# A two-layer decoder trunk: the order of instructions taken from the tool's time-line simulator

## The chip, the cores and the metric

The kernel is one program on one core of a Trainium2 chip. Its time is the device time of one execution in microseconds (us). TensorE (PE) multiplies, VectorE (DVE) and ScalarE (ACT) work on tiles in on-chip memory, GpSimd (POOL) does a little, and SyncE (SP) issues almost all transfers from the chip's main memory. Each engine takes its own instructions strictly in the order in which they were written into its list; between engines, semaphores make an instruction wait for what it needs. So an instruction that waits holds up all that stand behind it on its engine.

## The reference, cut to what matters

```python
# x (1, 256, 2048), c (1, 2048); everything float32
for layer in range(2):
    mod = silu(c) @ ada_w[layer, 0] + ada_b[layer, 0]      # 2048 x 6144 per use, four uses
    shift, scale, gate = split(mod, 3)
    h = rms_norm(x) * (1 + scale) + shift
    y = mlstm_mixer(h, ...) if layer == 0 else rglru_mixer(h, ...)
    x = x + gate * y
    h, gate = ada_modulate(x, c, ada_w[layer, 1], ada_b[layer, 1])
    x = x + gate * (square(relu(h @ w1[layer])) @ w2[layer])   # 2048 x 8192 and back
return rms_norm(x) * final_g
# mlstm_mixer: h @ w_in gives q, k, v, an output gate o and two gate columns per head; 8 heads in
#   two chunks of 128 positions: decay weights from cumulative sums and running maxima of the gate
#   columns, scores q k^T times these weights, a state k^T v carried from chunk to chunk, a
#   denominator, an RMS norm per head; the result times sigmoid(o), @ w_out
# rglru_mixer: h @ w_in gives xb, gb; a causal convolution over 4 positions of xb; two gates per
#   block of 256 channels by small products; a linear recurrence over time; times gelu(gb); @ w_out
```

## The kernel before, in words

Activations lie transposed, 128 channels by 256 positions to a tile, 16 tiles for the model's width. Products run in a split form: a weight tile of 128 x 2048 (1 MB, `raw`) is loaded by SP into a pool of four buffers; ACT copies each half into a rounded high part (`whi`, L174) and DVE subtracts it to get the low part (`wlo`, L175), in pools of four halves each, so two weight tiles are split ahead of PE at most. Activations are split likewise into the two halves of a `pair` (L184 and L185, or L187 and L188). PE then multiplies high by high, high by low and low by high: `mm3` (L194 to L196, three matmuls of 128x256), `mm2` (L200, L201, one of 128x512 and one of 128x256) or `mmu` (L217 to L219). A `block` is one output tile: 16 channel tiles, 48 matmuls with `mm3`.

Beside this runs the conditioning: 192 tiles `adaraw` of about 1 MB, each reduced on DVE against the vector made from `c` (L127) to one column of shifts, scales or gates. They are spread over the program by pacing numbers in the code, and they use the same buffers as the weights or two extra ones.

The stages, in order of time: the norm of x and the first projection in five groups of channel tiles (`group`, L511; from group 1 on ACT first copies the partial sums back into PSUM at L526, and copies the result out at L537); the gate columns and their cumulative sums and maxima (L574 to L626), which are written to a small table in main memory (`rows_d`) and read back broadcast as one tile `MB` per head (L634); then the eight heads, with eight blocks of the output gate (`ogate`) placed among them by a table in the code; the output projection (the first four tiles together, `awoa`, then twelve blocks); the first MLP; the RG-LRU mixer, two of its eight channel blocks at a time; its output projection (`bwo`); the second MLP, and the last norm.

One head goes back and forth between the engines. ACT makes the weights `E` (L646) and `qw` (L652) from `MB`, and `kw` (L643) from PE's transposed key `kp`; PE makes the state `cp` (L661) which ACT copies to `Cn` (L664); PE makes `num` and `den` (L671 to L677); ACT scales and squares these (`hb` L685, `hsq` L688, `ad` L680), DVE takes a maximum (L681) and ACT squares it (L682); PE sums the squares (`hss` L693) and DVE adds (L695). After every second head the pair of heads is normed: a table load and a reciprocal root on ACT (`rsy`, L270), three steps and two products on DVE (L271 to L273, L727), and the split into `zhi` (ACT, L731) and `zlo` (DVE, L732), which the output projection reads. The buffers for these allow two heads to be under way.

In the RG-LRU mixer the small gate products `gacc` (L194 to L196 into the second PSUM pool of three buffers) are followed on ACT by `th` (L836), `aa` (L839) and `TT` (L841), a root (L860) and a Gelu (L862), each of these with a table load when the function set changes; then on DVE by L865 to L870 and the split into the pairs that `bwo` reads.

What sets the order: the program is written as if one instruction followed another, and the tool makes each engine's list from it at building time by a simulation in which ready instructions are taken by priority. The priority is the place in the program, moved up by 200 for the weight splits (L173) and by 50 for the conditioning tiles (L126), by 1000 for the first norms.

## Time and profile before

| what | value |
|---|---|
| time, median of 3 runs (lowest, highest) | 2244.34 us (2240.72, 2247.15) |
| time of the profiled execution | 2244.5 us |
| its span | 2242.8 us, so 1.7 us lie around the span |
| mean clock granted to TensorE | 0.989 of full |
| busy in the span: PE, DVE, ACT, POOL | 2181.7, 1722.3, 1286.1, 90.1 us |
| read from main memory | 596.93 MB, 267 GB/s over the span |

A busy PE is a PE with at least one matmul under way. Matmuls overlap, so that the mean duration of one (0.28 us for 128x256) is longer than the distance from start to start; where the text counts matmuls it uses distances or the number in a stretch. In the rows of waits and of the time line, the number in square brackets is the idle time of the engine just before the instruction, followed by what ended it.

### The profile page before, as it was taken

The numbers are of one execution on the slowest core, as the hardware profiler recorded it, in microseconds if no ns is written. First come the engines' busy times: TensorE is split into PE (matmuls) and PEld (weight loads), VectorE is DVE, ScalarE is ACT, GpSimd is POOL, SyncE is SP. The second block draws the span as 40 slices with busy tenths as digits, with TensorE's granted clock in tenths as the row PEclk, the third lists the DMA queues.
The fourth block names the chain that finished last, engine by engine and source line by source line (L and its number), as shares of the span: only waits on it lengthen the run. The fifth ranks groups of instructions, "written<-read, shape, count | busy, mean of one in ns | idle before, by whom it ended". The sixth has DMA issues, their size and how long they took to land.

```text
span 2242.8 us, 34191 instructions
## 1 busy us (share of the span) xinstructions
PE 2181.7 (97%) x13606; PEld 1960.5 (87%) x13606; DVE 1722.3 (77%) x2199; ACT 1286.1 (57%) x1997; POOL 90.1 (4%) x70
## 2 busy tenths in 40 slices
PE   7899899899999999999999999999999999999998
PEld 6798799788888889888889999889888889888887
DVE  6777888988898788888889988998875555555554
ACT  6677777345674335665445877756664334665443
POOL 0000010220000000000110000020000000000110
PEclk9999999899999999999999999999999999999999
DMA  8888887897788999998997665776875555555552
GB/s 345 348 325 319 307 300 255 303 337 270 285 284 319 337 322 332 328 334 319 322 335 276 211 229 208 269 276 238 307 284 203 188 188 188 188 188 188 189 188 93
DMA packets 88671, 601.25 MB, mean 268 GB/s; under 512 B 10424, under 2 KB 14648, under 8 KB 16192
## 3 DMA queue, kind: packets, MB, share of 16 engines
q1 hardware_dynamic: 86400, 598.03, 74.3%
q8 instruction: 106, 1.74, 0.3%
q10 hardware_dynamic: 2112, 1.05, 0.2%
q14 instruction: 53, 0.43, 0.1%
HBM read 596.93 MB, written 2.11 MB: 267 GB/s over the span
## 4 chain that ended last, share of the span: by engine, by line
PE 86%; DVE 7%; ACT 3%; issue 2%; DMA 1%; SPq 0%; DVEq 0%; ACTq 0%
PE mm L200 42%; PE mm L201 22%; PE mm L511 8%; DVE wlo L175 3%; PE mm L196 2%; PE mm L195 2%; PE mm L194 2%; DVE adaraw L127 2%; ACT whi L174 1%; PE mm L218 1%; PE mm L217 1%; PE mm L219 1%; DMA adaraw<-in_ada 1%; PE mm L357 0%; DVE hmod L311 0%
## 5 line engine op out<-in xcount | busy, mean ns | idle before, releaser
L200 PE MATMUL mm<-pair,whi 128*128 128x512 f32 x4272 | 1496.3, 394 | 5.0 <-DVE pair L188 3.2
L201 PE MATMUL mm<-pair,wlo 128*128 128x256 f32 x4272 | 1195.9, 280 | 0.8 <-DVE wlo L175 0.8
L175 DVE TENSOR_TENSOR wlo<-raw,whi 128x1024 fp32r<-128x1024 f32 x736 | 900.2, 1233 | 380.1 <-ACT whi L174 375.9
L174 ACT ACTIVATE whi<-raw 128x1024 fp32r<-128x1024 f32 x736 | 771.9, 1057 | 609.7 <-PE mm L200 476.7
L200 PEld LDWEIGHTS mm<-pair,whi 128*128 128x128 f32 x4272 | 802.6, 188 | 190.7 <-DVE pair L188 4.7
L201 PEld LDWEIGHTS mm<-pair,wlo 128*128 128x128 f32 x4272 | 804.7, 188 | 1.7 <-DVE wlo L175 1.1
L127 DVE SCALAR_TENSOR_TENSOR adaraw<-adaraw,cbc 128x2050 f32<-128x2050 f32 x192 | 439.7, 2291 | 50.7 <-DMA adaraw<-in_ada 41.7
L511 PE MATMUL mm<-pair,whi 128*128 128x256 f32 x736 | 136.0, 288 | 10.7 <-ACT pair L187 5.7
L511 PEld LDWEIGHTS mm<-pair,whi 128*128 128x128 f32 x736 | 115.8, 194 | 12.9 <-ACT pair L187 6.3
L194 PE MATMUL mm<-pair,whi 128*128 128x256 f32 x432 | 123.1, 285 | 0.0
L195 PE MATMUL mm<-pair,whi 128*128 128x256 f32 x432 | 122.0, 282 | 0.0
L196 PE MATMUL mm<-pair,wlo 128*128 128x256 f32 x432 | 121.4, 281 | 0.0
L511 PE MATMUL mm<-pair,wlo 128*128 128x256 f32 x368 | 104.0, 288 | 2.9 <-DVE wlo L175 2.9
L336 DVE SCALAR_TENSOR_TENSOR xall<-mm,mod,xall 128x256 f32<-128x256 f32 x170 | 81.0, 480 | 27.0 <-PE mm L201 18.7
L378 ACT ACTIVATE hsum<-hsum 128x256 f32<-128x256 f32 x121 | 49.2, 413 | 81.7 <-DVE hsum L261 71.3
L291 POOL TENSOR_TENSOR nacc<-nacc,nsq 128x256 f32<-128x256 f32 x52 | 75.6, 1453 | 351.0 <-ACT nsq L282 350.7
L196 PE MATMUL mm<-zhi,wlo 128*128 128x256 f32 x256 | 75.8, 296 | 6.6 <-DVE wlo L175 6.6
L194 PEld LDWEIGHTS mm<-pair,whi 128*128 128x128 f32 x432 | 81.9, 190 | 0.4
L194 PE MATMUL mm<-zhi,whi 128*128 128x256 f32 x256 | 74.9, 297 | 7.6 <-ACT zhi L731 5.5
L195 PEld LDWEIGHTS mm<-pair,whi 128*128 128x128 f32 x432 | 81.8, 189 | 0.0
L196 PEld LDWEIGHTS mm<-pair,wlo 128*128 128x128 f32 x432 | 81.8, 189 | 0.0
L511 PE MATMUL mm<-whi,pair 128*128 128x512 f32 x256 | 81.0, 394 | 0.0
(218 smaller groups left out, 2054.7 us busy)
## 6 DMA issues: line engine op xcount, KB each, us to landing
raw<-in_w SPq DMA_DIRECT2D x220, 1024.0 KB, 5.1
adaraw<-in_ada SPq DMA_DIRECT2D x192, 1025.0 KB, 6.6
raw<-in_wqkv SPq DMA_DIRECT2D x40, 1024.0 KB, 8.5
raw<-in_w1a SPq DMA_DIRECT2D x32, 1024.0 KB, 6.2
raw<-in_bwi SPq DMA_DIRECT2D x28, 1024.0 KB, 5.0
raw<-in_bwo SPq DMA_DIRECT2D x16, 1024.0 KB, 5.1
raw<-in_awo SPq DMA_DIRECT2D x12, 1024.0 KB, 5.5
raw<-in_wo SPq DMA_DIRECT2D x8, 1024.0 KB, 6.2
```

Of the source, the lines that this page charges most:

```text
L127: V.scalar_tensor_tensor(out=raw, in0=raw, scalar=1.0, in1=cbc, op0=ALU.mult, op1=ALU.mult, accum_out=mod[i][:, j:j + 1])
L174: A.activation(hi, sl, AF.Copy)
L175: V.tensor_tensor(out=lo, in0=sl, in1=hi.bitcast(F32), op=ALU.subtract)
L194: PE.matmul(out, lhsT=whi, rhs=hi, start=first, stop=False)
L195: PE.matmul(out, lhsT=whi, rhs=lo, start=False, stop=False)
L196: PE.matmul(out, lhsT=wlo, rhs=hi, start=False, stop=last)
L200: PE.matmul(out, lhsT=whi, rhs=p.rearrange("p a t -> p (a t)"), start=first, stop=False)
L201: PE.matmul(out[:, 0:S], lhsT=wlo, rhs=p[:, 0, :], start=False, stop=last)
L291: G.tensor_tensor(out=self.acc, in0=self.acc, in1=sq, op=ALU.add)
L336: V.scalar_tensor_tensor(out=xT[j], in0=acc[:, a:a + S], scalar=mod[i][:, 32 + j:33 + j], in1=xT[j], op0=ALU.mult, op1=ALU.add)
L378: A.activation(h, h, AF.Relu, bias=c)
L511: PE.matmul(out, lhsT=l, rhs=m, start=clear and kk + n == 0, stop=kk == gn - 1 and n == len(ops) - 1, skip_group_check=True)
```

## The change

The context in which the program is written gets one argument. It selects the other of the two simulators that the tool has for ordering: one that keeps queues and transfers on a time line. Instructions, tiles, buffers, pools and priorities are the same; only the order in each engine's list differs, and with it the places where ACT needs a new function table (40 loads instead of 37).

```diff
-    with tile.TileContext(nc) as tc:
+    with tile.TileContext(nc, schedule_with_timeline_sim=True) as tc:
         trunk_kernel(tc, *args)
```

Of PE's 13426 instructions 10585 stand at the same place in both lists; of DVE's 2009 it is 729, of ACT's 1997 it is 113, of SP's 586 it is 497. The MLPs, most of the time, have nearly the same order on PE. The larger moves are in the first projection, in the heads and at the end of the RG-LRU mixer.

SP, between the first group of the projection and the second (`raw` are weight tiles, `adaraw` conditioning tiles; a piece of the difference, with - for before and + for now):

```order
+L161 DMA raw_341<-in_wqkv 128x2048
+L161 DMA raw_386<-in_wqkv 128x2048
+L161 DMA raw_434<-in_wqkv 128x2048
 L125 DMA adaraw_338<-in_ada 128x2050
-L161 DMA raw_341<-in_wqkv 128x2048
 L125 DMA adaraw_383<-in_ada 128x2050
-L161 DMA raw_386<-in_wqkv 128x2048
+L161 DMA raw_531<-in_wqkv 128x2048
+L161 DMA raw_595<-in_wqkv 128x2048
 L125 DMA adaraw_428<-in_ada 128x2050
+L161 DMA raw_662<-in_wqkv 128x2048
 L125 DMA adaraw_431<-in_ada 128x2050
```

Weight tiles move ahead of conditioning tiles: before the last of the conditioning tiles that the second group needs (adaraw_503, the 24th transfer before), there now stand four more weight tiles.

PE, at the state of head 0 (`cp_2791`; mm_2796 and mm_3392 are output-gate blocks, the second and the seventh of eight). Before:

```order
L194 MATMUL mm_2796<-pair_233,whi_2799 128x256
L195 MATMUL mm_2796<-pair_233,whi_2799 128x256
L196 MATMUL mm_2796<-pair_233,wlo_2800 128x256
L661 MATMUL cp_2791<-v0_195,kw_2778 128x256
L662 MATMUL cp_2791<-ones_85,kw_2778 128x128
L194 MATMUL mm_2796<-pair_513,whi_2799 128x256
L195 MATMUL mm_2796<-pair_513,whi_2799 128x256
```

Now:

```order
L194 MATMUL mm_3392<-pair_2287,whi_3399 128x256
L195 MATMUL mm_3392<-pair_2287,whi_3399 128x256
L196 MATMUL mm_3392<-pair_2287,wlo_3400 128x256
L661 MATMUL cp_2791<-v0_195,kw_2778 128x256
L662 MATMUL cp_2791<-ones_85,kw_2778 128x128
L671 MATMUL num_2859<-E_2780,v0_195 128x128
L672 MATMUL num_2859<-E_2780,v1_196 128x128
L675 MATMUL den_2866<-E_2780,ones_85 128x128
```

`cp_2791` is PE's row 1255 before and row 1546 now: six output-gate blocks that lay among the heads stand ahead of head 0, and one (mm_3522) is left among them. The reads of `MB` come later with them: on SP, five weight tiles and five conditioning tiles that stood behind the write of `rows_d` now stand ahead of it, and one weight tile and two conditioning tiles, where there was one conditioning tile, between it and the first `MB`.

PE, at the first product of the RG-LRU mixer's output projection that reads the last blocks' results (`pair_14156`; mm_14166, mm_14219, mm_14275 and mm_14328 are the first four output tiles). Before:

```order
L200 MATMUL mm_14275<-pair_13536,whi_14282 128x512
L201 MATMUL mm_14275<-pair_13536,wlo_14283 128x256
L200 MATMUL mm_14275<-pair_13543,whi_14282 128x512
L200 MATMUL mm_14166<-pair_14156,whi_14173 128x512
L201 MATMUL mm_14166<-pair_14156,wlo_14174 128x256
L200 MATMUL mm_14219<-pair_14156,whi_14226 128x512
```

Now:

```order
L200 MATMUL mm_14328<-pair_14142,whi_14335 128x512
L201 MATMUL mm_14328<-pair_14142,wlo_14336 128x256
L200 MATMUL mm_14328<-pair_14149,whi_14335 128x512
L201 MATMUL mm_14328<-pair_14149,wlo_14336 128x256
L200 MATMUL mm_14166<-pair_14156,whi_14173 128x512
L201 MATMUL mm_14166<-pair_14156,wlo_14174 128x256
```

Between the last of the gate products (gacc_13999) and this place stood 94 matmuls before, and 40 now; the gate products have moved back behind the blocks that used to follow them.

## The prediction

> **What bounds the kernel now.** I read the page first: busy shares, then the chain of work that ended last.
>
> ```profile
> PE 2181.7 (97%) x13606; PEld 1960.5 (87%) x13606; DVE 1722.3 (77%) x2199; ACT 1286.1 (57%) x1997; POOL 90.1 (4%) x70
> PE 86%; DVE 7%; ACT 3%; issue 2%; DMA 1%; SPq 0%; DVEq 0%; ACTq 0%
> ```
>
> PE is idle for 2242.8 - 2181.7 = 61.1 us in all. No instruction is added or removed but three table loads on ACT, so the change can win at most those 61 us and what they cost in clock, and loses wherever the new order makes PE wait. The table of stretches says where PE has room:
>
> ```profile
> core 0: us, PE busy (x) PEld busy (x) DVE busy (x) ACT busy (x) POOL busy (x), PEclk, DMA share, GB/s
> 20.00:80.00 60.00, 48.46 (x281) 43.58 (x282) 44.19 (x48) 34.13 (x53) 0.00 (x0) 0.89 0.90 360
> 400.00:450.00 50.00, 42.85 (x307) 42.35 (x308) 45.25 (x59) 19.66 (x40) 14.04 (x8) 0.83 0.84 299
> 450.00:500.00 50.00, 47.21 (x379) 46.70 (x378) 44.40 (x46) 20.58 (x27) 11.49 (x6) 0.97 0.94 346
> 600.00:1200.00 600.00, 600.00 (x3474) 526.95 (x3473) 513.12 (x606) 312.42 (x475) 18.90 (x13) 1.00 0.90 322
> 1230.00:1430.00 200.00, 198.69 (x1430) 185.11 (x1429) 177.09 (x308) 159.71 (x248) 0.00 (x0) 1.00 0.64 221
> 1450.00:2200.00 750.00, 749.78 (x4446) 663.75 (x4445) 476.49 (x584) 397.49 (x597) 26.51 (x24) 1.00 0.63 217
> ```
>
> From 600 to 1200 and from 1450 to 2200 PE never waits, at full clock, and its order hardly changes: nothing to win or lose there. The idle time lies before 510 us. The mixer at 1230 to 1430 runs without idle time, yet DVE is at 177 and ACT at 160 of 200 us: what its order hides now can come to light. The larger waits one by one, from the time line:
>
> ```profile
> 70.03 0.58 PE L511 MATMUL mm<-pair,whi 128*128 128x256 f32 x1 [4.69 <-ACT pair L187]
> 245.28 0.51 PE L200 MATMUL mm<-pair,whi 128*128 128x512 f32 x1 [1.74 <-ACT whi L174]
> 264.15 0.58 PE L511 MATMUL mm<-pair,whi 128*128 128x256 f32 x1 [4.79 <-ACT mm L526]
> 298.14 0.79 PE L661 MATMUL cp<-v,kw 128*128 128x256 f32 x1 [2.24 <-ACT kw L643]
> 401.77 0.58 PE L194 MATMUL mm<-zhi,whi 128*128 128x256 f32 x1 [5.55 <-ACT zhi L731]
> 435.28 0.58 PE L196 MATMUL mm<-zhi,wlo 128*128 128x256 f32 x1 [4.06 <-DVE wlo L175]
> ```
>
> After such a wait the clock falls, also after the one of 2.24 us (the number after POOL's is the granted clock):
>
> ```profile
> 298.00:301.40 3.40, 3.26 (x13) 3.08 (x14) 0.11 (x1) 1.66 (x4) 0.00 (x0) 0.50 0.91 303
> 410.60:420.00 9.40, 9.40 (x82) 9.40 (x81) 9.03 (x11) 6.64 (x16) 3.89 (x3) 1.00 0.72 242
> ```
>
> A stretch of 3.4 us at 0.50 costs 1.7 us. The last row gives the full-clock distance from one 128x256 matmul to the next, 9.40 / 82 = 0.115 us; a block of 48 is 5.5 us.
>
> **The change part by part.** *Second projection group.* Its first products wait for the conditioning tiles:
>
> ```profile
> GB/s 363 440 423 397 345 319 388 431 448 337 363 363 130 0 104 181 397 363 380 414 388 268 397 363 155 95 414 440 423 405 414 440 414 423 432 432 423 423 414 449
> 67.15 2.29 DVE L127 SCALAR_TENSOR_TENSOR adaraw<-adaraw,cbc 128x2050 f32<-128x2050 f32 x1
> ```
>
> The rates are of 38 to 76 us, in 40 slices. Four more 1 MB tiles ahead of the last conditioning tile are, at some 425 GB/s, 4 x 2.46 = 9.8 us. But the slices at 130, 0, 104, 181, 155 and 95 show about 5 us in which nothing much arrives, because SP waits for a buffer; with weights first, that pause is partly filled. I take 9.8 - 5.3 = **+4.5**, bounds 0 and 9.8. At the very start DVE's norm steps slip in between conditioning tiles, worth **-0.5** of the first wait.
>
> *From the third group to the last one (240 to 267).* The gate columns' weight tile is loaded and split earlier, and ACT copies partial sums (L526) ahead of the weight splits. That takes away 1.74 and most of 4.79, with one half-clock stretch each: at most 1.74 + 4.79 + 2 x 1.7 = 9.9 us. Small waits of 3 to 4 us take their place by the new order on ACT. **-6**, bounds -10 and -1.
>
> *The heads, the largest term.* State `cp` of head 0 is 291 matmuls later on PE. So 291 x 0.115 = 33.5 us of cover have been spent before the heads begin. Before, from 298.14 to 401.77, the heads took 103.6 us. To break even they must now take 70.1. ACT's work in that stretch, from the groups of 285 to 420 us:
>
> ```profile
> L685 ACT ACTIVATE hb<-num,halfg 128x256 f32<-128x256 f32 x16 | 6.7, 465 | 2.3 <-PE num L673 2.2
> L646 ACT ACTIVATE E<-MB,gT 128x128 f32<-128x128 f32 x16 | 5.8, 398 | 1.6 <-PE num L672 1.0 <-DMA MB<-rows_d 0.5
> L270 ACT ACT_TABLE_LOAD x4 | 5.1, 1283 | 0.1
> L731 ACT ACTIVATE zhi<-th 128x512 fp32r<-128x512 f32 x8 | 4.9, 622 | 2.7 <-DVE th L727 2.7
> L688 ACT ACTIVATE hsq<-num 128x512 f32<-128x512 f32 x8 | 4.8, 602 | 0.0
> L664 ACT ACTIVATE Cn<-cp 128x384 f32<-128x384 f32 x8 | 3.9, 488 | 7.2 <-PE cp L662 7.2
> L681 DVE SCALAR_TENSOR_TENSOR em<-em,ad 128x256 f32<-128x256 f32 x8 | 3.4, 420 | 0.3 <-ACT ad L680 0.3
> L656 ACT ACTIVATE em<-MB 128x256 f32<-128x256 f32 x8 | 3.3, 414 | 2.4 <-DVE rs L695 2.4
> L682 ACT ACTIVATE em<-em 128x256 f32<-128x256 f32 x8 | 3.3, 411 | 0.3 <-DVE em L681 0.3
> L652 ACT ACTIVATE qw<-MB 128x128 f32<-128x128 f32 x8 | 3.2, 397 | 0.0
> L680 ACT ACTIVATE ad<-den 128x256 f32<-128x256 f32 x8 | 3.1, 382 | 0.5 <-PE den L677 0.5
> L711 ACT ACT_TABLE_LOAD x2 | 2.6, 1283 | 0.0
> L711 ACT ACTIVATE th<-mm 128x256 f32<-128x256 f32 x8 | 3.0, 374 | 3.3 <-PE mm L196 3.3
> L643 ACT ACTIVATE kw<-kp,wk 128x128 f32<-128x128 f32 x8 | 3.0, 370 | 1.2 <-PE kp L641 1.2
> L270 ACT ACTIVATE rsy<-rs,tinyb 128x512 f32<-128x512 f32 x4 | 2.9, 726 | 0.0
> L174 ACT ACTIVATE whi<-raw 128x1024 fp32r<-128x1024 f32 x31 | 32.5, 1057 | 20.5 <-PE mm L195 14.2 <-DMA raw<-in_awo 6.0
> ```
>
> The nine ACT groups of the heads without table loads and splits (hb, E, hsq, Cn, both em, qw, ad, kw: 37.1 us) make 4.6 us a head; the table loads 5.1 + 2.6, rsy 2.9, zhi 4.9 and th 3.0 make 18.5; ten half weight tiles at 1.057 are 10.6. That is 66 us: if ACT never waited, the heads would now take 66, and the change would win 4. But a head is a loop in which ACT waits: for `cp`, for `num` and `den`, for DVE's maximum, for `hss`. Before, a block of 5.5 us lay beside each of these trips; now only one block and pieces of the projection lie there, and each piece needs an earlier pair's zhi. I put the trips at 2.5 us a head (an estimate: 0.42 on DVE, and short matmuls with their handovers for the rest). So a pair of heads takes 2 x (4.6 + 2.5) + 18.5 / 4 + 10.6 / 4 = 21.5, four pairs 86. PE's list also has the first product of the projection, which waits for the first pair's zhi, ahead of the next head's `hss` and `cp`, and on DVE two conditioning tiles (2.29 each, the L127 row) stand in that chain behind a table load, rsy and a table load (1.28 + 0.73 + 1.28): 2 x 2.29 + 3.3 = 8 us in which nothing goes on. 86 + 8 = 94, so **+24**; bounds 66 - 70 = -4, and +30 when every pair but the last has such a wait of some 2 us more. The later read of `MB` (ten more 1 MB transfers ahead of the table's write) lies beside the six blocks and costs nothing; without them it would be 25 us. Two or three more half-clock stretches than before: **+3** (0 to 5).
>
> *Output projection (402 to 510).* DVE is busy 45 of 50 us there, and PE waits for wlo (the 435.28 row). While PE stands in the heads, DVE does four conditioning tiles ahead that lay here before: 4 x 2.29 = 9.2 us less. The wait of 4.06, the 2.79 that PE lacks in 450 to 500, and a half-clock stretch behind each, are about 10 us; I take half back, **-5** (0 to -9).
>
> *RG-LRU.* Only the end pays in my reading. The chain from the last gate products to the last pair, before:
>
> ```profile
> 1416.09 0.47 ACT L836 ACTIVATE th<-gacc,hbra 128x256 f32<-128x256 f32 x1 [0.24 <-PE gacc L196]
> 1422.54 1.28 ACT L860 ACT_TABLE_LOAD   x1
> 1423.84 0.63 ACT L860 ACTIVATE TT<-TT 128x512 f32<-128x512 f32 x1
> 1427.57 2.29 DVE L127 SCALAR_TENSOR_TENSOR adaraw<-adaraw,cbc 128x2050 f32<-128x2050 f32 x1
> 1434.45 0.42 DVE L185 TENSOR_TENSOR pair<-gb,pair 128x256 fp32r<-128x256 f32 x1
> ```
>
> From 1416.09 to 1434.87 it took 18.8 us. Without the conditioning tile in it, 16.5. Now 40 matmuls and six of the last gate product lie beside it: 40 x 0.169 (749.78 / 4446, stretch 1450 to 2200) + 0.7 = 7.5 us. PE waits 9, and a half-clock stretch follows: some **+10**, bounds +3 (a chain of 10.3: from the first th to the root's end, 8.4 by the rows, then a table load and a Gelu of the same lengths, 1.9; no half clock) and 18.8 - 7.5 + 1.7 = 13. The three more table loads are 3 x 1.28 on an ACT with 40 of 200 us free: **+1** with other small waits of the mixer, bounds 0 and 4.
>
> The Trainium skill, ScalarE: Activation LUTs, "What ACT_TABLE_LOAD costs", adds about 1.38 us of drain to each load. By it the heads' eight loads and the two in this chain would cost 10 x 1.38 = 13.8 us more, and the sum would come to 2288 (an estimate from the page). The trace disagrees: the load at 1422.54 ends at 1423.82, and the root starts at 1423.84.
>
> **Sum**, against the profiled execution: 2244.5 + 4.5 - 0.5 - 6 + 24 + 3 - 5 + 10 + 1 = 2275.5; rounded down for the cover that my walk through the heads may have missed, **2274 us**. The profiled execution is 0.2 above the median of the three runs, so nothing is to be corrected.
>
> **The rivals.**
>
> *The order is hidden anyway* (within 0.3%, 6.7 us, which is about what a measurement of this kernel can tell from no change). ACT and DVE run ahead during the six blocks, and the heads come near ACT's floor: -4 to +4 instead of +24 + 3. Then 2244.5 + 4.5 - 0.5 - 6 + 0 - 5 + 10 + 1 = 2248. For it: ACT's 66 us are spread over 103.6 now. Against it: only two heads can be prepared. Chance 0.12.
>
> *Faster.* The same floor, and DVE's lead removes the waits of the output projection (-9), while the last gate chain is covered (+3): 2244.5 + 0 - 0.5 - 10 - 4 - 9 + 3 + 0 = 2224; with the middle values of the first two terms 2233. For it: the waits are really there, 61 us in all. Against it: PE's list has the heads bare. Chance 0.12.
>
> *Slower still*: every trip of the heads outlasts about 2 us, and PE's clock halves behind each. Eight heads with a wait above the 2.24 of the row at 298.14, at 1.7 each, are 13.6 instead of 3, and the mixer's middle gets its 4: 2274 + 10.6 + 3 = 2288; with the upper bounds of group two and the heads, 2299. For it: half clock stands behind 2.24 already. Against it: by my estimate a trip is 2.5 us for ACT, and PE works in a part of it. Chance 0.18. The Trainium skill, TensorE: Matmul & The Clock Gate, "What's actually happening", has the clock fall only after an idle window of about 3.4 us. By it these trips would cost no clock, and the sum would be 2271; the trace disagrees for single waits (2.24 at 298.14, half clock from 298.0 to 301.4), so I keep the rival.
>
> *Transfers.* Weights ahead of conditioning tiles could fill the queue, so that later groups wait, +5 more at 80 to 240. The stretch 20 to 80 has DMA at 0.90, so it may bind; it is inside the range.
>
> **How the numbers follow.** Likeliest: 0.58 for 2274, whose own range is 2258 to 2290. With the rivals: faster 0.13, same 0.11, slower 0.76. The range from 2240 to 2299 leaves out the larger wins and the worst of the losses.
>
> **What would show it.** In the profile after: PE's share of the heads' stretch, with waits for kw, Cn, E or zhi summing to 30 to 40 us; a first wait of about 8 us for the first pair's zhi; the wait at 70 moved by 4 to 5 us and the waits at 245 and 264 gone; a wait of some 9 us for the last pair before the mixer's output projection; fewer waits for wlo between the heads and the first MLP; nothing new in the MLPs. I am wrong if the time from head 0's state to the last pair's zhi is under 80 us, or if the last gate chain is hidden.

## The result and the profile after

The changed kernel takes **2307.06 us** (median of 4 runs, 2304.93 to 2308.94). The kernel before took 2245.74 (4 runs, 2240.72 to 2251.46) beside it. The ratio is 1.027, with a 95% interval of 1.0247 to 1.0294: slower by 61 us, where 30 were forecast (2274, range 2240 to 2299). The profiled execution has a span of 2303.6 us. Busy shares, the chain that ended last and the conditioning tiles' group, from the page after:

```profile
PE 2199.1 (95%) x13606; PEld 1972.5 (86%) x13606; DVE 1715.9 (74%) x2199; ACT 1297.1 (56%) x2000; POOL 69.3 (3%) x70
PE 78%; DVE 7%; DMA 7%; ACT 5%; issue 3%; SPq 0%; DVEq 0%; ACTq 0%
L127 DVE SCALAR_TENSOR_TENSOR adaraw<-adaraw,cbc 128x2050 f32<-128x2050 f32 x192 | 440.8, 2296 | 125.9 <-DMA adaraw<-in_ada 116.5
```

The same group of conditioning tiles before:

```profile
L127 DVE SCALAR_TENSOR_TENSOR adaraw<-adaraw,cbc 128x2050 f32<-128x2050 f32 x192 | 439.7, 2291 | 50.7 <-DMA adaraw<-in_ada 41.7
```

PE is idle for 2303.6 - 2199.1 = 104.5 us, against 61.1 before: 43.4 of the 61 us are new waits. The chain that ended last, in which transfers had 1%, now gives them 7%, and DVE stands 125.9 us ahead of conditioning tiles instead of 50.7. The clock of each core (span, then the mean clock granted to TensorE), first after, then before:

```profile
core 0: 2303.6 us, clock 0.978
```
```profile
core 0: 2242.8 us, clock 0.989
```

2303.6 x 0.022 = 51 and 2242.8 x 0.011 = 25 us of full clock are missing. Half clock is granted in stretches, so that is about 102 and 50 us at half clock. Only the part in which PE works costs time. With PE's gaps and the stretch behind its last matmul left out, that part cost 32.2 us after and 18.3 before: **14.0 us** more. 43.4 + 14.0 = 57.4 of 60.8 us between the two profiles. The other 3 to 4 us no wait in the trace shows.

PE's waits, largest sums first (line, releaser: us in total, times, longest), after:

```profile
PE mm L194 <- ACT zhi L731: 24.9, 4, 8.3
PE mm L511 <- ACT pair L187: 9.9, 2, 6.7
PE mm L511 <- ACT hdirect L316: 8.4, 1, 8.4
PE mm L201 <- DVE wlo L175: 6.4, 7, 1.9
PE mm L200 <- DVE pair L188: 5.9, 3, 3.3
PE kp L641 <- ACT ad L680: 4.5, 2, 2.3
PE bc L113 <- DVE sc L109: 3.7, 1, 3.7
PE gacc L194 <- ACT th L836: 3.6, 1, 3.6
PE num L673 <- ACT Cn L664: 3.0, 2, 2.2
```

Where it went by stage needs the same milestones in both: the last product of the first projection (L511), the last `zhi` of the heads (L731), and the last residual step (L336) of the output projection, of the first MLP and of the RG-LRU mixer. The windows between them (length, busy and count of PE, weight loads, DVE, ACT, POOL, clock, DMA share, GB/s) are, of before, heads, output projection and RG-LRU mixer:

```profile
288.70:401.77 113.07, 103.46 (x816) 100.13 (x814) 95.42 (x124) 76.26 (x145) 9.13 (x8) 0.98 0.79 284
401.77:488.30 86.53, 78.36 (x591) 77.45 (x592) 77.69 (x87) 34.07 (x58) 25.53 (x14) 0.89 0.88 320
1209.49:1510.54 301.05, 299.67 (x2070) 276.30 (x2069) 272.88 (x462) 220.98 (x352) 17.27 (x14) 1.00 0.67 237
```

and of the changed kernel:

```profile
281.07:432.90 151.83, 113.68 (x817) 107.88 (x815) 112.34 (x150) 79.17 (x148) 3.40 (x8) 0.87 0.68 245
432.90:506.40 73.50, 73.47 (x603) 73.27 (x604) 64.89 (x77) 35.11 (x58) 15.65 (x14) 0.97 0.84 307
1236.84:1564.67 327.83, 308.20 (x2067) 283.00 (x2066) 270.71 (x464) 224.17 (x355) 17.45 (x14) 0.97 0.62 219
```

The 816 matmuls of the heads, the same but for one or two, take 113 us in one order and 152 in the other. Every stage so, with PE's gaps added up and what half clock cost while PE was busy:

| stage | before, us | after, us | difference | of it waits | of it clock | forecast |
|---|---|---|---|---|---|---|
| start to the last L511 | 288.7 | 281.1 | -7.6 | -1.9 | -1.4 | -2 |
| to the last zhi: heads | 113.0 | 151.8 | +38.8 | +28.5 | +9.0 | +27 |
| to the last residual of the output projection | 86.6 | 73.6 | -13.0 | -8.2 | -6.3 | -5 |
| first MLP, to its last residual | 721.2 | 730.4 | +9.2 | +4.3 | +2.7 | 0 |
| RG-LRU mixer, to its last residual | 301.1 | 327.8 | +26.8 | +18.2 | +8.3 | +11 |
| rest, with the second MLP | 732.2 | 738.9 | +6.7 | +2.3 | +1.7 | 0 |

The waits of the heads one by one, from PE's time line after (start, duration, what, idle before and its releaser):

```profile
354.18 0.58 PE L194 MATMUL mm<-zhi,whi 128*128 128x256 f32 x1 [6.65 <-ACT zhi L731]
371.97 0.38 PE L673 MATMUL num<-qw,Cn 128*128 128x128 f32 x1 [2.19 <-ACT Cn L664]
378.71 0.39 PE L194 MATMUL mm<-zhi,whi 128*128 128x256 f32 x1 [3.50 <-ACT zhi L731]
400.53 0.33 PE L641 MATMUL kp<-ident,qk 128*128 128x128 f32 x1 [2.21 <-ACT ad L680]
407.29 0.58 PE L194 MATMUL mm<-zhi,whi 128*128 128x256 f32 x1 [6.42 <-ACT zhi L731]
432.90 0.58 PE L194 MATMUL mm<-zhi,whi 128*128 128x256 f32 x1 [8.34 <-ACT zhi L731]
```

All four pairs of heads now end in a wait for their `zhi`, of 3.5 to 8.3 us, where before one did (5.55). In the last of them DVE has ended the norm's third step at 427.78 and starts the two products for `zhi` at 431.50; between stands a conditioning tile, for whose transfer it waits first:

```profile
429.28 2.29 DVE L127 SCALAR_TENSOR_TENSOR adaraw<-adaraw,cbc 128x2050 f32<-128x2050 f32 x1 [1.50 <-DMA adaraw<-in_ada]
```

That is 3.7 of the 8.34 us. The RG-LRU mixer, whose longest wait was 0.41 us, now has

```profile
1295.50 0.39 PE L194 MATMUL mm<-pair,whi 128*128 128x256 f32 x1 [2.64 <-ACT whi L174]
1396.37 0.58 PE L194 MATMUL gacc<-pair,ghi 128*128 128x256 f32 x1 [3.63 <-ACT th L836]
1473.30 0.39 PE L201 MATMUL mm<-pair,wlo 128*128 128x256 f32 x1 [1.88 <-DVE wlo L175]
1496.95 0.50 PE L200 MATMUL mm<-pair,whi 128*128 128x512 f32 x1 [1.40 <-ACT whi L174]
```

and a dozen smaller ones; no single large one.

### The profile page after: what moved, and what is told of

Same layout as the page of the kernel before. It is cut to its first block, busy times and chain, and to the rows that moved or that the text cites. A ratio compares the mean times of both kernels' runs of the same rounds, so it can differ in the third digit from the quotient of the medians.

```text
span 2303.6 us, 34199 instructions
## 1 busy us (share of the span) xinstructions
PE 2199.1 (95%) x13606; PEld 1972.5 (86%) x13606; DVE 1715.9 (74%) x2199; ACT 1297.1 (56%) x2000; POOL 69.3 (3%) x70
## 4 chain that ended last, share of the span: by engine, by line
PE 78%; DVE 7%; DMA 7%; ACT 5%; issue 3%; SPq 0%; DVEq 0%; ACTq 0%
PE mm L200 38%; PE mm L201 19%; PE mm L511 9%; DMA adaraw<-in_ada 6%; PE mm L194 3%; PE mm L196 3%; PE mm L195 3%; DVE adaraw L127 2%; DVE wlo L175 2%; ACT whi L174 1%; PE mm L219 1%; PE mm L218 1%; PE mm L217 1%; DVE hmod L311 1%; DVE pair L188 0%
## 5 line engine op out<-in xcount | busy, mean ns | idle before, releaser
L127 DVE SCALAR_TENSOR_TENSOR adaraw<-adaraw,cbc 128x2050 f32<-128x2050 f32 x192 | 440.8, 2296 | 125.9 <-DMA adaraw<-in_ada 116.5
L511 PE MATMUL mm<-pair,whi 128*128 128x256 f32 x736 | 133.7, 285 | 12.4 <-ACT pair L187 9.9
L511 PEld LDWEIGHTS mm<-pair,whi 128*128 128x128 f32 x736 | 114.6, 192 | 14.2 <-ACT pair L187 10.4
L511 PE MATMUL mm<-pair,wlo 128*128 128x256 f32 x368 | 102.5, 284 | 0.0
L336 DVE SCALAR_TENSOR_TENSOR xall<-mm,mod,xall 128x256 f32<-128x256 f32 x170 | 80.8, 479 | 23.2 <-PE mm L201 20.8
L194 PE MATMUL mm<-zhi,whi 128*128 128x256 f32 x256 | 73.9, 296 | 24.9 <-ACT zhi L731 24.9
L511 PE MATMUL mm<-whi,pair 128*128 128x512 f32 x256 | 81.2, 395 | 0.0
L217 PE MATMUL mm<-unnormed,whi 128*128 128x258 f32 x272 | 77.3, 285 | 0.0
L219 PE MATMUL mm<-unnormed,wlo 128*128 128x258 f32 x272 | 76.8, 284 | 0.5 <-DVE wlo L175 0.5
L218 PE MATMUL mm<-unnormed,whi 128*128 128x256 f32 x272 | 77.0, 284 | 0.0
```

Of the source, the lines that this page charges most:

```text
L127: V.scalar_tensor_tensor(out=raw, in0=raw, scalar=1.0, in1=cbc, op0=ALU.mult, op1=ALU.mult, accum_out=mod[i][:, j:j + 1])
L194: PE.matmul(out, lhsT=whi, rhs=hi, start=first, stop=False)
L217: PE.matmul(out[:, 0:UX], lhsT=whi, rhs=u[:, 0:UX], start=first, stop=False)
L218: PE.matmul(out[:, 0:S], lhsT=whi, rhs=u[:, UX:UW], start=False, stop=False)
L219: PE.matmul(out[:, 0:UX], lhsT=wlo, rhs=u[:, 0:UX], start=False, stop=last)
L511: PE.matmul(out, lhsT=l, rhs=m, start=clear and kk + n == 0, stop=kk == gn - 1 and n == len(ops) - 1, skip_group_check=True)
```

## The experiments

**Theory 1** is the prediction's: the waits come from the order inside a stage, and a stage carries its loss wherever it stands. **Theory 2**: the loss is one of the whole program (transfers shifted at the start, all stages late for them). **Theory 3**, formed after the result: the conditioning tiles `adaraw`, which now stand further forward on DVE and wait there for their transfers, hold up what is behind them. **Theory 4**: half clock behind the waits is a cost of its own.

The tool for most of them is the kernel before, in which an engine's order within a stage is taken from the changed kernel. Two neighbours of a stored list get an edge that orders them and does nothing else:

```diff
+def pin(tc):
+    nosync = mybir.DependencyInfo(mybir.DependencyClass.NoSync, mybir.DependencyReason.DATA)
+    by_name = {i.name: i for i in tc.nc.cur_bb.bb.instructions}
+    for _, packed in ORDERS:
+        n, last = 0, None
+        for d in json.loads(zlib.decompress(base64.b85decode(packed))):
+            n += d
+            ins = by_name.get(f"I-{n}")
...
+            if last is not None:
+                tc.add_manual_dep(ins, last.name, nosync, reason="order")
+            last = ins
...
         trunk_kernel(tc, *args)
+        pin(tc)
```

The diffs below give the lists in `ORDERS`, or the rows of a list that were moved. Instructions are cut into stages by their place in the program, so at a border two lists can slide past each other.

### One stage at a time

The first projection alone:

```diff
-first projection: lists of before
+first projection: lists of the changed kernel (PE, ACT, DVE, SP)
 all later stages: lists of before
```

> The kernel before, with the changed order in the first projection only (everything up to the gate columns); all other stages keep the order of before. The trace of the changed kernel reaches the end of this stage 7.6 us earlier than before. If the stages act each by itself (theory 1): 8 us faster, about 2237, with the waits at 245 and 264 gone and the one at 70 moved to 77. If what is won there is only lent, because the next stage's conditioning tiles are later (theory 2): 0 to 3 us faster. The sum of the prediction had 2 us faster for this stage.

Measured: 2246.34 us beside 2245.85, ratio 1.0004 (0.9993 to 1.0015). Nothing. The stage ends at 287.4 us, where before it ended at 288.7 and in the changed kernel at 281.1. Against the expectation, the wait in the last group is still there:

```profile
262.83 0.58 PE L511 MATMUL mm<-pair,whi 128*128 128x256 f32 x1 [4.79 <-ACT mm L526]
```

The last group's order belongs to the lists of the next run.

The heads alone (gate columns, last group, all eight heads):

```diff
-gate columns, last group and heads: lists of before
+gate columns, last group and heads: lists of the changed kernel
 all other stages: lists of before
```

> The kernel before, with the changed order in the gate columns, the last projection group and the eight heads only. Theory 1, the stages act each by itself: 39 us slower for this stage, of which the output projection gives some 11 back because DVE has done its conditioning tiles ahead: 2245 + 28 to 39, about 2278. Theory 2, the loss of the later stages comes from the state in which the heads leave the buffers and the conditioning tiles: the whole of 61 us and more, about 2306. The sum of the prediction had 27 us for this stage, less 5.

Measured: 2275.61 beside 2245.85, ratio 1.014 (1.0123 to 1.0157): +30 us. The first projection now ends at 285.0. From `cp` of head 0 to the last `zhi` it is 95.0 us, close to the forecast's 94.

The first MLP alone:

```diff
-first MLP: lists of before
+first MLP: lists of the changed kernel
```

> The kernel before, with the changed order in the first MLP only. PE's order is nearly unchanged there, DVE's is not: conditioning tiles stand in front of weight splits and DVE waits for their transfers. Theory 1: 10 to 14 us slower, about 2257, with DVE's idle time before conditioning tiles up from 42 to some 75 us. Theory 2, the MLP's loss comes from earlier stages: no change. The sum of the prediction had nothing for this stage.

Measured: 2257.44 beside 2245.85, ratio 1.0055 (1.004 to 1.007): +11.6 us, in a stage in which "nothing new" was forecast.

The RG-LRU mixer with its output projection alone:

```diff
-RG-LRU mixer and its output projection: lists of before
+RG-LRU mixer and its output projection: lists of the changed kernel
```

> The kernel before, with the changed order in the RG-LRU mixer and its output projection only. Theory 1: 21 us slower, about 2266, with waits of about 3.6 us at the gate products in the middle and a row of waits of 1 to 2 us before the output projection. Theory 2, part of that comes from earlier stages: 10 us or less. The sum of the prediction had 11 us for this stage.

Measured: 2275.99 beside 2245.85, ratio 1.0139 (1.0118 to 1.016): +30 us where 21 were expected, with 18.6 us of waits and 7.2 of clock in the stage.

The second MLP alone:

```diff
-second MLP: lists of before
+second MLP: lists of the changed kernel
```

> The kernel before, with the changed order in the second MLP only. If the 7 us that the trace shows there come from its order: 5 to 7 slower, with waits of 0.9 and 1.7 us for the norm's pairs at the MLP's start. If they are the spread of runs (rival): within 2 us.

Measured: 2248.8 beside 2244.56, ratio 1.0016 (1.0 to 1.0032): +4, hardly outside of nothing. Between profiles with the same list this stage differs by as much (+4.9 with the heads' lists alone).

What follows: Theory 1 holds and Theory 2 falls, since the heads, the first MLP and the RG-LRU mixer each bring their loss with them. 0.5 + 29.8 + 11.6 + 30.1 + 4.2 = 76 us, more than the 61 of all together. What the output projection gives back is missing from that sum; with it (26.4 for both, the next run, instead of 29.8) the sum is 73. The other 12 us are not explained: the stages' losses do not simply add.

The heads with the output projection:

```diff
-gate columns, last group, heads and output projection: lists of before
+gate columns, last group, heads and output projection: lists of the changed kernel
```

> The kernel before, with the changed order in the gate columns, the heads and the output projection together. With the heads alone changed it was 2275.6. If the conditioning tiles that the changed order draws from the output projection into the heads only move a cost (theory 1): the heads take 13 us longer than with the heads alone changed (108 instead of 95 from head 0's state to the last pair's zhi), the output projection gives 8 to 11 back, 2272 to 2278. If they cost more than they give back: 2285 and more.

Measured: 2271.35 beside 2244.93, ratio 1.0112 (1.0093 to 1.0131): +26. The heads are longer than in the run with the heads alone (148.3 us, 37.0 idle, instead of 138.8), and the output projection takes 72.8 instead of 85.3. So most of its gain only returns what the heads lost. What moved is DVE's work: by the last `zhi` it has done 128 conditioning tiles, as in the changed kernel, where the run with the heads alone and the kernel before have done 119.

### Which engine's list, in the heads

```diff
+PE: list of the changed kernel in the heads
 PE in the output projection: list of before; DVE, ACT, POOL, SP in both: ordered anew by the first simulator
```

> The kernel before, with the changed order in the heads on PE alone (six output-gate blocks ahead of head 0); the other engines' lists are made anew for it by the first simulator. If the cover that is spent ahead is the cause (theory 1): 20 to 35 us slower, as with all engines of the heads changed (30). If it is the order on DVE and ACT inside the heads (rival): 10 us or less.

Measured: 2255.71 beside 2244.93, ratio 1.0044 (1.0027 to 1.0062): +11, between the two expectations.

```diff
+PE, ACT: lists of the changed kernel in the heads and the output projection
 DVE, POOL, SP there: ordered anew by the first simulator
```

> TensorE's and ScalarE's changed order in the heads and the output projection; VectorE, GpSimd and SyncE are ordered anew by the first simulator; every other stage has the order of before. The changed order of all engines there gave +26 us, TensorE's alone +11. Theory A (ScalarE's order makes the missing 15 us: weight splits and conversions stand between the steps of a head): +22 to +28 here, heads of 143 us or more, TensorE idle in them 30 us or more. Theory D (VectorE's order makes it: conditioning tiles and low weight parts stand in the chain): +8 to +15 here, idle about 20 us. Both together: between, +16 to +21, here and in the run beside this one.

Measured: 2266.46 beside 2243.3, ratio 1.0096 (1.0079 to 1.0114): +22 to +23.

```diff
+PE, DVE: lists of the changed kernel in the heads and the output projection
 ACT, POOL, SP there: ordered anew by the first simulator
```

> TensorE's and VectorE's changed order in the heads and the output projection; ScalarE, GpSimd and SyncE are ordered anew by the first simulator; every other stage has the order of before. Theory A (ScalarE's order makes the 15 us that TensorE's order alone doesn't): +8 to +15 here, TensorE idle in the heads about 20 us. Theory D (VectorE's order makes them): +22 to +28, idle 30 us or more. If neither run reaches +16, it is SyncE's order, the arrival of weights and tiles, or all of them only together.

Measured: 2285.6 beside 2243.3, ratio 1.0186 (1.0171 to 1.0202): +42, more than with all lists. PE's waits for `zhi` in three of these kernels, in the order of the runs above:

```profile
PE mm L194 <- ACT zhi L731: 6.6, 2, 4.4
```
```profile
PE mm L194 <- ACT zhi L731: 21.1, 4, 7.8
```
```profile
PE mm L194 <- ACT zhi L731: 31.8, 4, 10.0
```

With PE's and ACT's lists the four waits of the changed kernel are there (21.1 of 24.9 us). DVE's list isn't needed for them, and with an ACT list that was not made for it, it costs 19 us more than ACT's list with a DVE list made to fit. So the losses of single lists don't add; that lists made together fit each other is how I read it. One thing is not told apart: the first of these runs left PE's list in the output projection as before, the other two did not, so the step from +11 to +22 is ACT's list and PE's second stage together.

### Conditioning tiles in the chains (Theory 3)

In the heads, seven tiles were moved from inside a pair's norm chain (L271 to L732) to behind it, on DVE, once with the changed lists of heads and output projection:

```diff
-L127 SCALAR_TENSOR_TENSOR adaraw,mod_128<-adaraw,cbc 128x2050
 L653 SCALAR_TENSOR_TENSOR qw<-qk_189,qw 128x128
 L273 SCALAR_TENSOR_TENSOR rs<-rsu,rsy 128x512
-L127 SCALAR_TENSOR_TENSOR adaraw,mod_128<-adaraw,cbc 128x2050
 L727 TENSOR_TENSOR th<-th,rs 128x512 x2
-L127 SCALAR_TENSOR_TENSOR adaraw,mod_128<-adaraw,cbc 128x2050
 L732 TENSOR_TENSOR zlo<-th,zhi 128x512 x2
+L127 SCALAR_TENSOR_TENSOR adaraw,mod_128<-adaraw,cbc 128x2050 x3
...
```

> The kernel with the changed order in the heads and the output projection (2271.4), and one thing undone: the seven conditioning tiles that stand on DVE between the first step of a pair's norm (L271) and its last split (L732) stand behind it. If these tiles hold up the chain that PE waits for (theory 1): the waits for zhi of 7.5, 3.2, 6.6 and 8.0 us shrink by about 2.3 us for each tile, 10 to 16 us in all, 2255 to 2261. If PE waits for ACT's table loads and the heads' own trips (rival): 3 us or less.

and once with the order of before:

```diff
 L271 SCALAR_TENSOR_TENSOR rsu<-rs,rsy 128x512
-L127 SCALAR_TENSOR_TENSOR adaraw,mod_128<-adaraw,cbc 128x2050
 L272 SCALAR_TENSOR_TENSOR rsu<-rsu,rsy 128x512
...
-L127 SCALAR_TENSOR_TENSOR adaraw,mod_128<-adaraw,cbc 128x2050
-L732 TENSOR_TENSOR zlo<-th,zhi 128x512
+L732 TENSOR_TENSOR zlo<-th,zhi 128x512 x2
+L127 SCALAR_TENSOR_TENSOR adaraw,mod_128<-adaraw,cbc 128x2050 x2
```

> The kernel before, with the same one thing: seven conditioning tiles on DVE move from the inside of a pair's norm chain to behind it. Theory 1: the wait of 5.5 us for the last pair's zhi shrinks by some 4 us and a half-clock stretch with it: 2245 - 4 to 8, about 2239, faster than both kernels. Rival, the tiles are then in the way of the output projection's weight splits: no change.

Measured: 2279.59 beside 2246.07, ratio 1.0149 (1.0126 to 1.0172), which is 7 to 8 us worse than without the move; and 2253.6 beside 2246.07, ratio 1.0036 (1.002 to 1.0053), 7.5 us worse, where 4 to 8 us faster were expected. PE's waits from 290 to 520 us, changed lists with the tiles moved, then without:

```profile
PE mm L194 <- ACT zhi L731: 15.7, 4, 5.5
PE mm L196 <- DVE wlo L175: 8.4, 5, 5.0
PE den L675 <- DVE rs L695: 5.5, 1, 5.5
```
```profile
PE mm L194 <- ACT zhi L731: 25.4, 4, 8.0
PE mm L196 <- DVE wlo L175: 0.9, 2, 0.7
```

The chain does get shorter (25.4 to 15.7), as forecast. But the three tiles then stand in one block of 3 x 2.29 us ahead of the next weight split and of the next head's `rs`, and the wait is there. In the heads, then, Theory 3 is right about the chain and wrong about the time: taken out of the chain, the tiles cost no less at the next wait, on a DVE that is busy 73.6 of the 105.0 us from `cp` of head 0 to the last `zhi` in the kernel without the move.

In the mixer the same (12 tiles moved by up to eight places):

```diff
-L127 SCALAR_TENSOR_TENSOR adaraw,mod_130<-adaraw,cbc 128x2050
 L175 TENSOR_TENSOR wlo<-raw,whi 128x1024
+L127 SCALAR_TENSOR_TENSOR adaraw,mod_130<-adaraw,cbc 128x2050
...
```

> The kernel with the changed order in the RG-LRU mixer and its output projection on all engines (2276), and one thing undone: on DVE its twelve conditioning tiles move back by up to eight instructions, past weight splits and past the mixer's own chain. If the tiles in front of the chain are the cause (theory 1): 8 to 15 us come back, 2261 to 2268, mostly at the end of the mixer, where one tile waits 3.2 us for its transfer. If the order of ACT and of the activations' splits is the cause (rival): 4 us or less come back.

Measured: 2274.89 beside 2246.07, ratio 1.0137 (1.011 to 1.0164), the same as the 1.0139 without the move. Moving the tiles brings nothing of the mixer's loss back. PE's list alone, with all other engines ordered anew by the first simulator:

```diff
+PE: list of the changed kernel in the RG-LRU mixer and its output projection
 DVE, ACT, POOL, SP there: ordered anew by the first simulator
```

> The kernel before, with the changed order of the RG-LRU mixer and its output projection on PE alone; the other engines' lists are made anew for it by the first simulator. With all engines it was 2276, 30 us slower. If the late gate products on PE are the cause (the prediction's step): 20 us or more slower, with a wait of about 9 us at the end. If it is what stands ahead of the weight splits and of the last chain on ACT and DVE (rival): 10 us or less.

Measured: 2276.05 beside 2246.07, ratio 1.0135 (1.0112 to 1.0158): all of the +30, though not by the expected wait of about 9 us at the end: the longest is 3.77. So in the mixer PE's list is enough for the loss. In that list all 32 gate products stand 35 to 93 places later; 199 of the other 1874 matmuls have another place among themselves too. That it is the gate products is read from this and was not tested apart. How much of it is the end:

```diff
-last pair of blocks and output projection: lists of before
+last pair of blocks and output projection: lists of the changed kernel
 rest of the RG-LRU mixer: lists of before
```

> The kernel before, with the changed order in the last pair of blocks of the RG-LRU mixer and its output projection only. The prediction put 10 of the mixer's 11 us there. By the traces, of the 30 us of the whole mixer some 9 come before the second pair, 5 to 7 in the middle: 10 to 15 slower than before, about 2257. If the end is only late because the earlier blocks are (rival): 5 or less.

Measured: 2262.49 beside 2244.56, ratio 1.0079 (1.0063 to 1.0096): +18 of the 30 (10 to 15 were expected), with 9.8 us of waits and 4.8 of clock in the stage, where one wait of 9 and 1.7 of clock were forecast.

In the first MLP the tiles do matter. The groups of DVE's tiles and weight splits in its second half, before (850 to 1200 us) and after (870 to 1230), the same work:

```profile
L175 DVE TENSOR_TENSOR wlo<-raw,whi 128x1024 fp32r<-128x1024 f32 x125 | 154.2, 1238 | 24.9 <-ACT whi L174 22.8 <-PE mm L201 1.8
L127 DVE SCALAR_TENSOR_TENSOR adaraw<-adaraw,cbc 128x2050 f32<-128x2050 f32 x47 | 107.6, 2290 | 25.0 <-DMA adaraw<-in_ada 24.8
```
```profile
L175 DVE TENSOR_TENSOR wlo<-raw,whi 128x1024 fp32r<-128x1024 f32 x125 | 152.0, 1217 | 8.1 <-ACT whi L174 7.9
L127 DVE SCALAR_TENSOR_TENSOR adaraw<-adaraw,cbc 128x2050 f32<-128x2050 f32 x48 | 110.1, 2293 | 53.0 <-DMA adaraw<-in_ada 52.8
```

DVE stands 53 us instead of 25 before tiles whose transfer has not landed, and the splits behind wait for nothing of their own any more (8 instead of 25). On DVE's time line after:

```profile
1145.47 2.29 DVE L127 SCALAR_TENSOR_TENSOR adaraw<-adaraw,cbc 128x2050 f32<-128x2050 f32 x1 [2.55 <-DMA adaraw<-in_ada]
1147.69 1.22 DVE L175 TENSOR_TENSOR wlo<-raw,whi 128x1024 fp32r<-128x1024 f32 x1
```

The order of before, with only those tiles moved on DVE that the changed kernel has further forward, each to ahead of the same weight split:

```diff
 L311 SCALAR_TENSOR_TENSOR hmod<-xall,mod_128,nrstd 128x256
+L127 SCALAR_TENSOR_TENSOR adaraw,mod_128<-adaraw,cbc 128x2050
 L175 TENSOR_TENSOR wlo<-raw,whi 128x1024 x2
 L188 SCALAR_TENSOR_TENSOR pair<-hmod,mod_128,pair 128x256
...
-L127 SCALAR_TENSOR_TENSOR adaraw,mod_128<-adaraw,cbc 128x2050
 L175 TENSOR_TENSOR wlo<-raw,whi 128x1024
```

> The kernel before, with one thing changed: in the first MLP, on DVE, each conditioning tile stands ahead of the same weight split as in the changed order (mostly one place earlier). If DVE's wait for a conditioning tile's transfer, with a ready weight split behind it, is the MLP's loss (theory 1): 9 to 13 us slower, as with the whole order of the first MLP (11.6), and DVE's idle time before conditioning tiles up by 25 us or more. If it is something else in that order (rival: ACT's order, the norm's steps): no change.

Measured: 2271.65 beside 2244.93, ratio 1.0112 (1.009 to 1.0133): +27, more than the 11.6 of all lists. PE's waits and the tiles' group over its whole span (idle time 50.7 before):

```profile
PE mm L201 <- DVE wlo L175: 14.7, 14, 6.8
```
```profile
L127 DVE SCALAR_TENSOR_TENSOR adaraw<-adaraw,cbc 128x2050 f32<-128x2050 f32 x192 | 439.6, 2291 | 89.7 <-DMA adaraw<-in_ada 89.5
```

So this step alone is enough for such a loss, and more; the other moves of the changed kernel must soften it. How long DVE waits does not set the loss: with all lists of the first MLP it stands 97.5 us ahead of tiles, longer than here, and the loss is 11.6. The opposite test takes the changed kernel, and puts 119 tiles that stand directly ahead of a weight split directly behind it:

```diff
-L127 SCALAR_TENSOR_TENSOR adaraw,mod_127<-adaraw,cbc 128x2050
 L175 TENSOR_TENSOR wlo<-raw,whi 128x1024
+L127 SCALAR_TENSOR_TENSOR adaraw,mod_127<-adaraw,cbc 128x2050
...
```

> The changed kernel, with one thing changed: on DVE each conditioning tile that stands directly ahead of a weight split stands directly behind it (119 of 192 tiles). Theory 1: the first MLP's 12 us come back and some of the mixer's, 2307 - 12 to 20 = 2287 to 2295. Rival, these waits are only where DVE would wait anyhow: 2307.

Measured: 2311.96 beside 2244.93, ratio 1.0295 (1.0277 to 1.0312), 5 us above the changed kernel, with intervals that overlap (1.0247 to 1.0294 there); in any case not the 12 to 20 us that were to come back. The first MLP becomes 5.4 us shorter (730.4 to 725.0) and PE's 2.6 us of waits for `wlo` in it are gone, as Theory 3 has it; the first projection is 6.3 us longer (281.1 to 287.4), perhaps because a tile that is worked off later gives its buffer back later, which was not tested. Theory 3 is borne out for the first MLP, by about half of its loss, and not as a cure for the program.

### Half clock by itself (Theory 4)

Into the kernel before, 25 products with a tile of ones go into a tile that nobody reads, ahead of the waits at 70, 402 and 435 us, so that PE works while it waits. The orders of both kernels are kept by lists:

```diff
                 idle(IDLE, ob[-1][:, 0, :])
+                idle(8, cbc[:, 0:S])
...
             w = weights(awoa_d[kg])
+            if kg == 3:
+                idle(10, cbc[:, 0:S])
...
         for j in range(KC):
+            if j == 8:
+                idle(7, cbc[:, 0:S])
```

> The kernel before, with the same order, and 25 extra products of ones into a spare tile placed in three of PE's waits: 8 ahead of the wait of 4.7 us at 70, 10 ahead of the one of 5.5 at 402, 7 ahead of the one of 4.1 at 435 (about 0.43 us each, less than the wait). Theory, the half clock is a cost of its own: the half-clock stretches behind these waits (6.8, 10.2 and 6.8 us) go or shorten, 4 to 10 us faster, about 2238. Rival, the other engines set the pace there: within 2 us of before.

and into the changed kernel 17 ahead of the waits at 68 and 77 and 15 ahead of the one at 433:

```diff
                 idle(IDLE, ob[-1][:, 0, :])
+                idle(17, cbc[:, 0:S])
...
             w = weights(awoa_d[kg])
+            if kg == 3:
+                idle(15, cbc[:, 0:S])
```

> The changed kernel, with the same order, and 32 such products: 5 and 12 ahead of the waits of 3.1 and 6.8 us at 68 and 77, 15 ahead of the one of 8.3 us at 433. Theory, the half clock is a cost of its own: the stretches of 13.7 us from 68.6 and of 10.2 us from 427 shorten, 5 to 10 us faster than 2307. Rival, other engines set the pace: within 2 us.

Measured: **2240.2** (12 runs) beside 2244.56 (23), ratio 0.9981 (0.9969 to 0.9993), faster than both kernels of this case; and 2302.14 (2292.15 to 2306.6) beside 2244.56, ratio 1.0251 (1.0227 to 1.0275), 5 us below 2307, with an interval that overlaps the changed kernel's (1.0247 to 1.0294), so that a gain there isn't shown. The stretches round the two places in the kernel before, without and with the products (with them the second place comes 5 us earlier; the profiled execution took 2234.7 us, less than the median):

```profile
60.00:80.00 20.00, 13.74 (x87) 12.97 (x86) 12.32 (x14) 8.33 (x12) 0.00 (x0) 0.83 0.95 387
395.00:445.00 50.00, 39.07 (x276) 38.36 (x275) 45.42 (x60) 18.68 (x39) 12.04 (x8) 0.83 0.85 307
```
```profile
60.00:80.00 20.00, 17.25 (x124) 15.88 (x125) 14.09 (x16) 10.59 (x16) 0.00 (x0) 1.00 0.93 380
390.00:440.00 50.00, 46.99 (x365) 45.38 (x364) 49.16 (x63) 21.39 (x42) 14.39 (x9) 1.00 0.87 323
```

The clock goes from 0.83 to 1.00, and in 20 and 50 us PE gets 37 and 89 more matmuls done. The 8 and 17 added products count twice in these rows, so 21 and 55 of them are the kernel's own. So half clock behind a wait is a cost of its own in the kernel before. In the changed kernel time at half clock falls from 102 to 80 us. Yet its heads, where the wait at 433 is filled, end no earlier (434.2 after 432.8 us): the last `zhi` comes from ACT and DVE, and a faster PE doesn't hurry it. What the clock alone costs the changed kernel in the heads was not measured apart from the waits.

## Why the prediction was wrong in size

The direction was right, and so were most of the stages: the heads, the end of the RG-LRU mixer, a gain at the last group, something back in the output projection. The sum was half of what came. Four of its steps failed: the half clock (4.7 us in heads and mixer, 17.3 measured), the waits of the later pairs of heads (put at nothing, 18.3 us), the mixer ahead of its end (+1, about 10 us of waits) and the first MLP (nothing, +9.2). The gains in the first projection and in the output projection were put too small as well, which offset part of that. Step by step:

- **Second projection group, +4.5 - 0.5.** At the 240th L511 product the change is 6.6 us behind (76.1 to 82.7), within the bounds. By the 1320th it has made up all but 0.7 of that, which the prediction had nothing on.
- **Third to last group, -6.** Right in kind: between products 1320 and 1380 the difference goes from +0.7 to -9.3, at the bound of -10. It is not a gain of the first projection's own lists, with which the wait of 4.79 us stays; with the lists of gate columns and heads it goes, in a run that loses 30 us in all. The six blocks that follow are work that PE has to do anyway; that ahead of the heads it only comes earlier, so that the gain is lent, is argued and not shown by a run.
- **Heads, +24.** The mechanism was right: "waits for kw, Cn, E or zhi summing to 30 to 40 us" came as 30.1 (38.1 with PE's other waits), and the first wait for zhi is 6.65 where 8 was written. The step that failed is the pair's chain: 8 us were put on the first pair and nothing on the later ones, whose waits for zhi are 3.50, 6.42 and 8.34. From `cp` of head 0 to the last `zhi` it is 108.1 us, forecast 94. With the heads' lists alone it is 95.0, but that is partly luck: ACT was busy 58 of these 95 us, where the estimate had 66. With the changed lists in the output projection too it is 105.0; nine more conditioning tiles then lie ahead of the last `zhi`, and each pair's first product is bound to its place. Which of the two makes the 10 us was not tested apart.
- **Half clock, +3 in the heads and 1.7 at the end.** This is the largest mis-sized term: +9.0 and +8.3 of the time in which PE works. The rival "slower still" had the price, 1.7 us behind each wait of about 2 us; it got a chance of 0.18, and its time of 2288 to 2299 was below the result too.
- **Output projection, -5.** It gave 13, its waits (8.3 to 0.1) and its half clock (8.5 to 2.2). "I take half back" was the error, and with it the lead of DVE: nine conditioning tiles (119 to 128 by the last `zhi`), not four. It was paid in the heads.
- **RG-LRU, +10 for the end and +1 for the rest.** One wait of 9 us was forecast. At the end a row of small ones came instead; that their sum is nearly the same (9.8 us in the run of the end alone) is luck. 4.8 us of clock came where 1.7 was written. Earlier in the mixer another 10 us of waits came, for which the prediction had "+1 with other small waits of the mixer". It costed that as ACT's table loads, while PE's list alone makes the whole loss.
- **The MLPs, nothing.** +9.2 in the first. The prediction looked at PE's list, which hardly moves there, and at PE never waiting. It did not look at DVE's list, on which a tile stands one weight split further forward, ahead of its transfer.

Both rules of the Trainium skill that the prediction weighed can be read again. The Trainium skill, ScalarE: Activation LUTs, "What ACT_TABLE_LOAD costs", adds a drain of about 1.38 us to each load. ACT's time line after shows none:

```profile
1461.10 1.28 ACT L860 ACT_TABLE_LOAD   x1
1462.39 0.63 ACT L860 ACTIVATE TT<-TT 128x512 f32<-128x512 f32 x1
```

The load ends at 1462.38 and the root starts at 1462.39, as before the change. The Trainium skill, TensorE: Matmul & The Clock Gate, "What's actually happening", has the clock fall after an idle window of about 3.4 us. The trace disagrees: in the mixer half clock follows two waits of 1.34 and 0.83 us (shown in the last section). By that rule the wait of 8.34 us at 433 would still halve the clock, and the row of small waits at the end of the mixer would cost none; it cost 4.8 us in the run of the end alone.

What stays open: the 3 to 4 us that no wait shows; the 12 us by which the stages' losses exceed the whole; why moving the tiles alone costs the first MLP 27 us and all its lists only 12; and how the heads' +26 divides between ACT's list and PE's. Shown are the stages' losses, PE's list as enough for the mixer's, the tiles as enough for a loss in the first MLP, and half clock as a cost of its own in the kernel before; that tiles ahead of their transfers make the changed kernel's 9 us in the first MLP is borne out by about half only.

## What to carry to other kernels

An order is costed stage by stage and on every engine: where PE's list stands still, look at whether an instruction on DVE or ACT has moved ahead of a transfer that it must wait for, since everything behind it on that engine waits too. Work that moves across a border takes its cost along: with nine conditioning tiles more in the heads these took 10 us longer and the output projection 12 us less. So measure to the next point at which the engines meet. Count each wait of about two microseconds on a busy PE with the half clock that can follow it, and try a few idle products in its place.

## What the runs showed of the hardware

The clock falls behind waits shorter than expected. On PE's time line after, and in the stretch from 1311 us (the number after POOL's is the clock):

```profile
1308.85 0.38 PE L194 MATMUL gacc<-pair,ghi 128*128 128x256 f32 x1 [1.34 <-ACT pair L184]
1310.29 0.39 PE L195 MATMUL gacc<-pair,ghi 128*128 128x256 f32 x1 [0.83 <-DVE pair L185]
```
```profile
1311.00:1314.40 3.40, 3.40 (x18) 3.34 (x16) 2.62 (x4) 1.94 (x5) 0.00 (x0) 0.50 0.79 304
```

Two waits, 2.17 us in a stretch of about 3, and then 3.4 us at 0.50 in which PE is busy all the time. Half clock comes in stretches of 3.4, 6.8, 10.2 or 13.7 us (17.1 once, with PE's and ACT's lists in the heads), multiples of 3.4, in every kernel here; only the last one of each trace, which runs past its end, is another length. In each trace all of them start on one grid of 3.41 us. Over all 20 profiles, from 30 us on, every step of that grid at full clock in which PE stood for more than 0.56 of the step was followed by half clock, and none in which it stood for less than 0.35; between the two both occurred. So a wait of 2 us may halve the clock or not, by how it lies on the grid and what waits lie beside it: in the kernel before, half clock followed the one of 2.03 us at 474.05 and did not follow the one of 2.04 at 503.39. During a long wait the clock falls within the wait:

```profile
427.00:432.90 5.90, 0.00 (x0) 0.00 (x0) 4.27 (x7) 0.68 (x2) 0.00 (x0) 0.50 0.20 61
```

The wait of 8.34 us that ends at 432.90 began at 424.56, and half clock is granted from 427.0 to 437.2. Plain products of ones kept the clock at 1.00 through the waits that they filled in the kernel before, and 25 of them won 4.4 us (1.6 to 7.0 by the interval).
